# A feed-forward that begins with its narrow column group instead of a wide one

## The chip, the cores and the metric

One NeuronCore of one Trainium2 chip runs the whole program. The metric is device time in microseconds (us) of one execution, lower is better. The engines are named as in the profile: PE is TensorE (matmuls; its weight loads are PEld), DVE is VectorE, ACT is ScalarE, POOL is GpSimd, SP is SyncE, which issues most of the DMAs.

## What is computed

Two decoder layers over 256 tokens of width 1024, in float32. The change touches the feed-forward alone, with `D_FF` = 2816 columns:

```python
def swiglu(h, w_gate_up, w_down):
    gu = h @ w_gate_up
    gate, up = jnp.split(gu, [D_FF], axis=-1)
    return (jax.nn.silu(gate) * up) @ w_down

...
        h = h + hybrid_mixer(rmsnorm(h, norm_mix_w[l]), w_in[l], ret_out[l], conv_w[l], conv_b[l],
                             dt_bias[l], a_log[l], d_skip[l], ssd_norm_w[l], ssd_out[l], w_o[l])
        h = h + swiglu(rmsnorm(h, norm_ffn_w[l]), w_gate_up[l], w_down[l])
```

The mixer ends with the product `merged @ w_o`, so the feed-forward's input is `h` plus that product, normalised.

## The kernel before

Every float32 product is made of three matmuls of a rounded type: each operand is split into a high part (`wh`, `xh`), which ScalarE rounds, and a low part (`wl`, `xl`), which VectorE gets by subtraction. `mm3` (lines 542 to 545) issues high by high, high by low, low by high. All weights go through this: a piece of 128 x 1024 elements is loaded by SP, rounded by ScalarE (line 506) and subtracted by VectorE (line 527). There are seven buffers for split pieces (`HB` = 7).

The 256 tokens are two tiles of 128, t0 and t1. The normalised input stands transposed in `xT`, in two halves of 512 features, each with its high and low part.

The 2816 columns of the feed-forward are groups `c` = 0 to 4 of 512 and group 5 (`NPAIR`) of 256, each for the gate and for the up product. There are three ways to compute a group:

- tokens stationary (`tm_jobs`, `tm_pair`, lines 824 and 859): the stationary operand is a block of `xT`, the weights stream past, the result has tokens as rows. A step `(m, t, k)` is one `mm3` for member `m` (0 gate, 1 up), token tile `t` and row block `k` of 8. The result has to be transposed on TensorE (`transposed`, line 631) for the product that follows.
- weights stationary (`fm_job`, line 970, lines 988 to 991): a block of weights is stationary and the high and low parts of all tokens stream past, 512 columns, then 256 columns against the low weights. The result is already transposed; its two halves are added by ScalarE and VectorE (`gathered`).
- "seven" (`wino_job`): a Strassen-like product with seven instead of eight blocks, tokens stationary, whose weight sums are made on VectorE and by DMAs. It needs sums of `xT`, which `seven_sums` makes on VectorE in the first part of the feed-forward (tiles `plain` and `D`).

The table `FFN` sets the order of the groups: tokens stationary for 0, then 1 (weights stationary), 2 (seven), 3 (weights stationary), 4 (seven), 5 (weights stationary), then the down projection `out_wino`. The first entry is not done by the general job but by `tm_pair`, whose order of steps is

```python
(m, t, k) for t in range(NT) for m, n in ((0, 8), (1, 4)) for k in range(n)
```

and after that the last four `k` of up for both tiles. So it begins with t0 alone: 8 steps of gate and 4 of up.

Ahead of it stands the output projection (`out_job` with `head=8 - TAIL`), which finishes one accumulator after another, that of t1's second half last. After each, `add_to(norm)` adds it to `h`; `Norm.half` makes the sum of squares (`square`: ScalarE, line 776), the reciprocal root (`power`: GpSimd, line 655), the normalised rows `xn` in a `sil` tile (VectorE, line 744, in the trace L233), their transposes (TensorE, line 640) and the split into `xT` (ScalarE, then VectorE). t1's part of this runs while the feed-forward's first matmuls of t0 do.

The order of instructions on each engine is fixed when the program is built: `Flow` is a small event model in the kernel that takes, on each engine, the ready operation with the lowest priority number, by costs and latencies written in it. The hardware then runs each engine's list in that order.

`gate_post` applies the silu to the gate (ScalarE), `up_post` multiplies by up (VectorE), transposes and splits into `gu`, the operand of the down projection, which asks for its groups in the order 0, 3, 4, 5, with the two groups 1 and 2 as a seven in between.

Of the kernel before, what the change touches and what calls it, by code (L numbers as in the profile page):

```python
# [11 lines left out]
AF = mybir.ActivationFunctionType  # L12
ALU = mybir.AluOpType
# [3 lines left out]
P = 128  # L17
D = 1024
SEQ = 256
NT = 2  # L20
# [7 lines left out]
NPAIR = FF // 512  # L28
C_Q, C_K, C_V, C_G, C_Z, C_X, C_DT, C_GR, C_GS = 0, 1024, 2048, 4096, 6144, 8192, 11264, 11296, 12320
NB = 24  # L30

GF = (1, 3, NPAIR)


DW = 1
# [157 lines left out]
def trunk_kernel(  # L193
# [8 lines left out]
    SLOW, MT_SLACK = 1500.0, 800.0  # L202
# [17 lines left out]
    def act(n, pr, out, in_, func, psum=False, **kw):  # L220
        ptr = sum(hasattr(kw.get(a), "shape") for a in ("scale", "bias"))
        cost = 0.833 * n + (50 if psum else 92) + 93 * ptr + (95 if "accum_out" in kw else 0)
        return Op("act", cost, lambda: nc.scalar.activation(out=out, in_=in_, func=func, **kw),  # L223
                  pr, TABLES.get(func))
# [4 lines left out]
    def tt(n, pr, out, in0, in1, op):  # L229
        return dve(n, pr, lambda: nc.vector.tensor_tensor(out=out, in0=in0, in1=in1, op=op))  # L230
# [593 lines left out]
    def tm_jobs(xT, members, order):  # L824

        first, pe_pr = take(len(members))
        acc, left = {}, {}
        for m, t, k in order:
            post, n, kper = members[m]
            j = first + m  # L830
            if k == 0:
                yield accS
            yield xT.when(k, t)
            wh, wl = yield jobs[j][k // kper]

            def emit():
                if not started[0]:
                    started[0] = True

                    idle[0].pr, idle[0].cost, idle[0].fn = -10, 0.0, lambda: None  # L840
                if k == 0:
                    acc[m, t] = new_acc()
                xh, xl, _ = xT.at(k // 4)
                tsl = slice(t * P, (t + 1) * P)
                mm3(acc[m, t][:, :n], xh[:, k % 4, tsl], xl[:, k % 4, tsl], wh[:, k % kper, :], wl[:, k % kper, :], k == 0, k == 7)

            yield pe(3 * mm_cost(n), pe_pr + 0.5, emit)
            left[m, k // kper] = left.get((m, k // kper), NT * kper) - 1
            if not left[m, k // kper]:
                fl.release(hlS)  # L850
            if k == 7:
                fl.spawn(post(t, acc[m, t], j, accS))
# [3 lines left out]
        return tm_jobs(xT, [(post, n, kper)], [(0, t, k) for t in range(NT) for k in range(lead)]  # L856
                       + [(0, t, k) for k in range(lead, 8) for t in range(NT)])

    def tm_pair(xT, *members):

        return tm_jobs(xT, members, [(m, t, k) for t in range(NT) for m, n in ((0, 8), (1, 4)) for k in range(n)]
                       + [(1, t, k) for k in range(4, 8) for t in range(NT)])

    GOT = ("a", "b", "c1", "c2", "u1", "u2", "u3")

# [191 lines left out]
    def out_wino(op, nk, at, tag, order, post, add, ops):  # L1057
# [74 lines left out]
        for t in range(NT):  # L1132
# [6 lines left out]

    FFN = [[("plain", 0)],
           [("fm", 1)],
           [("seven", (2,), ("t3", "t4"))],
           [("fm", 3)],
           [("seven", (4,), ("t3", "t4"))],
           [("fm", NPAIR)]]
    DIRECT = ()
    DOWN_APART = ()

# [14 lines left out]
    def add_layer_jobs(l):  # L1165
        def srcs_of(kind, *at):
            if kind == "gr":
                return tm_srcs(w_gr[l, at[0]])
            if kind in FM:
                return fm_srcs(w_fm[l, FM[kind] + at[0] + (at[0] + at[1] if len(at) > 1 else 0)])  # L1170
            if kind in ("ret", "ssd", "wo"):
                return out_srcs({"ret": ret_out, "ssd": ssd_out, "wo": w_o}[kind][l])
            return tm_srcs(w_tm[l, TM[kind] + at[0]], kper=1 if l == 0 and (kind, *at) == ("v", 0) else 2)

        def adds_of(kind, *at, order=MIXED):
            if kind == "seven":
                c = TM[at[0]] + at[1]
                return [sevens(w_tm[l, c], w_tm[l, c + 1], added=at[2], order=order, slots=None)]
            return [plain((srcs_of(kind, *at), APARTS.get((kind, *at), ())))]

        for m in MIXERS[l]:
            if m == ("ret",):
                group(sevens(w_rw[l, 0], w_rw[l, 1], added=("t3", "t4"), order=RMID, first=RET_FIRST),
                      plain((out_srcs(ret_out[l])[8:], RET_APART)))
            elif m == ("ssd",):
                group(sevens(w_sw[l, 0], w_sw[l, 1], added=("t3", "t4"), order=SMID, slots=(ccS, new_cc)),
                      plain((out_srcs(ssd_out[l])[8:], ())))
            elif isinstance(m, tuple):
                for add in adds_of(*m, order=ALONE):
                    group(add)  # L1190
            else:
                group(*(chain(*(a for j in stream for a in adds_of(*j))) for stream in m))
        for members in FFN:
            adds = []
            for kind, *at in members:
                if kind == "seven":
                    adds.append(chain(*(sevens(w_gate_up[l, 0, c], w_gate_up[l, 1, c], added=at[1], order=ALONE if len(members) == 1 else ASIDE,
                                               slots=(ccS, new_cc)) for c in at[0])))
                elif kind == "fm":
                    adds.append(plain(*((srcs, APART) for c in at for srcs in gf_srcs(l, c))))  # L1200
                else:
                    adds.append(plain(*((srcs, APART) for c in at for srcs in gate_up_srcs(l, c))))
            group(*adds)
        lone = [s for k, s in enumerate(out_srcs(w_down[l])) if k // 4 not in (DW, DW + 1)]
        group(sevens(w_dw[l, 0], w_dw[l, 1], added=("t3", "t4"), order=AMID, slots=(ccS, new_cc)),
              plain((lone, DOWN_APART)))
# [24 lines left out]
    def layer(l, mix, nxt, opening=None):  # L1231
# [696 lines left out]

        gu = Operand(NPAIR + 1, ["A", "C", "Y", "A", "C", "Y"])

        def gate_post(sg_ev):
            def post(t, ps, j, sem):
                yield silS
                s = new_sil()
                yield act(512, j, s, ps, AF.Silu, psum=sem is accS)
                fl.release(sem)
                fl.set(sg_ev[t], s)
            return post

        def up_post(sg_ev, c):  # L1940
            def post(t, ps, j, sem):
                s = yield sg_ev[t]
                yield tt(512, j, s, ps, s, ALU.mult)
                fl.release(sem)
                yield from transposed(s, 4, gu, c, t, j, slack=SLOW)
                fl.release(silS)
            return post

# [48 lines left out]
                makers += [((lambda p=p, job=job: job(ffn.xT, p)), 1) for p in (gate, up)]  # L1997
            return makers

        def pair(c):  # L2000
            sg_ev = [Event() for _ in range(NT)]
            return gate_post(sg_ev), up_post(sg_ev, c)

        def ffn_jobs(kind, *at):
            if kind == "seven":
# [5 lines left out]
        last = max(i for i, g in enumerate(FFN) for kind, *_ in g if kind == "seven")  # L2011
        for i, members in enumerate(FFN):
            if i == 0:
                yield from tm_pair(ffn.xT, *((m, 512, 2) for m in pair(members[0][1])))
            else:
                yield from together(*[ffn_jobs(*m) for m in members])
            if i == last:
                ffn.drop_sums()
# [202 lines left out]
```

## Time and profile before

| | before |
|---|---|
| time, median of 3 runs | 1253.2 us (1253.19 to 1253.69) |
| the profiled execution | 1253.21 us, span 1251.4 us |
| mean granted TensorE clock | 0.999 |
| PE busy | 1241.9 us, 99% |
| DVE busy | 1108.2 us, 89% |
| ACT busy | 882.7 us, 71% |
| DMA | 266.27 MB, mean 213 GB/s |

The span runs from the first to the last instruction; 1.8 us of the time lie outside it. A matmul's shown duration covers its way through the array and overlaps the next one, so the pace of matmuls is read from start to start. "Idle before, releaser" behind a row says how long the engine stood and which instruction ended that.

### The profile page before, as it was taken

Reading aid. Unit: us, or ns where it says so; the run is one execution under the profiler, and the core shown is the slowest. Engines: PE = TensorE matmul, PEld = TensorE weight load, DVE = VectorE, ACT = ScalarE, POOL = GpSimd, SP = SyncE. Lnnn points to the kernel's source line nnn. Section 1 sums busy time; section 2 is a strip of 40 time slices with the busy share of each in tenths; the row PEclk is TensorE's granted clock in tenths of the full one; section 3 lists DMA queues with packets and bytes.
Section 4 is the critical chain, followed back from the end, with each engine's and each line's share of the span. In section 5 each row is a group of like instructions: output and inputs, shape, how many; then the busy total and the mean of one; then the engine's idle time right before and its main releaser. Section 6 shows DMA issues by size and latency. Waiting matters only on the chain.

```text
span 1251.4 us, 17609 instructions
## 1 busy us (share of the span) xinstructions
PE 1241.9 (99%) x6286; PEld 1052.4 (84%) x6286; DVE 1108.2 (89%) x1516; ACT 882.7 (71%) x1305; POOL 71.1 (6%) x92
## 2 busy tenths in 40 slices
PE   9999999999999999999999999999999999999997
PEld 8889888888888888888888898888888888888886
DVE  6998989789999979999788888888899998899995
ACT  6866876977776666776586676878877674776753
POOL 0000000001012001001000000000010110010000
PEclk9999999999999999999999999999999999999999
DMA  8758555456768658877776475555577786688872
GB/s 293 248 146 284 184 180 174 153 194 192 253 238 226 229 178 231 297 212 219 249 257 227 124 256 167 188 172 163 208 186 234 243 234 213 225 209 249 289 204 86
DMA packets 76343, 266.27 MB, mean 213 GB/s; under 512 B 8768, under 2 KB 9024, under 8 KB 76256
## 3 DMA queue, kind: packets, MB, share of 16 engines
q1 hardware_dynamic: 68416, 237.25, 55.7%
q0 software_dynamic: 7552, 27.38, 11.8%
q8 instruction: 49, 0.80, 0.2%
q10 hardware_dynamic: 288, 0.52, 0.1%
q14 instruction: 38, 0.31, 0.1%
HBM read 262.96 MB, written 2.16 MB: 212 GB/s over the span
## 4 chain that ended last, share of the span: by engine, by line
PE 92%; ACT 3%; issue 2%; DMA 1%; DVE 0%; POOL 0%; SPq 0%; POOLq 0%; ACTq 0%
PE acc L543 19%; PE acc L544 19%; PE acc L545 19%; PE acc L988 15%; PE acc L989 9%; PE tr L640 2%; PE yps L1700 2%; PE acc L991 2%; ACT wh L506 1%; ACT seg L1668 1%; PE acc L1422 1%; PE tr L1593 1%; PE ips L1687 1%; DMA raw<-in_w_tm_dram 1%; DMA raw<-in_w_gr_dram 0%
## 5 line engine op out<-in xcount | busy, mean ns | idle before, releaser
L506 ACT ACTIVATE wh<-raw 128x1024 fp32r<-128x1024 f32 (+2 forms) x388 | 397.0, 1035 | 150.6 <-PE acc L545 36.3
L527 DVE TENSOR_TENSOR wl<-raw,wh 128x1024 fp32r<-128x1024 f32 (+2 forms) x388 | 458.9, 1196 | 48.5 <-ACT wh L506 46.6
L988 PE MATMUL acc<-xT,wh 128*128 128x512 f32 x840 | 304.2, 400 | 0.0
L989 PE MATMUL acc<-xT,wl 128*128 128x256 f32 x960 | 251.6, 281 | 0.0
L543 PE MATMUL acc<-wh,xT 128*128 128x512 f32 (+1 forms) x568 | 220.6, 388 | 0.0
L545 PE MATMUL acc<-wh,xT 128*128 128x512 f32 (+1 forms) x568 | 216.1, 380 | 0.0
L544 PE MATMUL acc<-wl,xT 128*128 128x512 f32 (+1 forms) x568 | 216.1, 380 | 0.0
L989 PEld LDWEIGHTS acc<-xT,wl 128*128 128x128 f32 x960 | 181.2, 189 | 10.1
L988 PEld LDWEIGHTS acc<-xT,wh 128*128 128x128 f32 x840 | 158.0, 188 | 32.2
L544 PEld LDWEIGHTS acc<-wl,xT 128*128 128x128 f32 x568 | 106.7, 188 | 20.4 <-issue 1.2
L543 PEld LDWEIGHTS acc<-wh,xT 128*128 128x128 f32 x568 | 106.7, 188 | 19.8 <-issue 1.6
L545 PEld LDWEIGHTS acc<-wh,xT 128*128 128x128 f32 x568 | 106.6, 188 | 19.5
L506 ACT ACTIVATE wh<-raws 128x1024 fp32r<-128x1024 f32 x80 | 83.5, 1056 | 31.7 <-DVE raws L230 12.5
L527 DVE TENSOR_TENSOR wl<-raws,wh 128x1024 fp32r<-128x1024 f32 x80 | 96.4, 1222 | 8.9 <-ACT wh L506 8.7
L543 PE MATMUL acc<-wh,A 128*128 128x512 f32 x224 | 89.8, 401 | 0.2
L545 PE MATMUL acc<-wh,A 128*128 128x512 f32 x224 | 87.4, 390 | 0.0
L544 PE MATMUL acc<-wl,A 128*128 128x512 f32 x224 | 87.3, 390 | 0.0
L233 DVE SCALAR_TENSOR_TENSOR cc<-cc,cv 128x255 f32<-128x255 f32 (+1 forms) x144 | 67.3, 479 | 3.0 <-ACT cc L223 2.1
L543 PE MATMUL acc<-wh,C 128*128 128x512 f32 (+1 forms) x152 | 59.2, 389 | 0.0
L544 PE MATMUL acc<-wl,C 128*128 128x512 f32 (+1 forms) x152 | 58.3, 384 | 0.2 <-DVE wl L527 0.2
L545 PE MATMUL acc<-wh,C 128*128 128x512 f32 (+1 forms) x152 | 58.2, 383 | 0.0
L223 ACT ACT_TABLE_LOAD x41 | 52.6, 1283 | 6.1 <-DVE cc L233 5.4
(197 smaller groups left out, 2006.8 us busy)
## 6 DMA issues: line engine op xcount, KB each, us to landing
raw<-in_w_tm_dram SPq DMA_DIRECT2D x104, 512.0 KB, 4.2
raw<-in_w_fm_dram SPq DMA_DIRECT2D x80, 512.0 KB, 4.3
raw<-in_w_gf_dram SPq DMA_DIRECT2D x40, 512.0 KB, 4.5
raw<-in_w_gate_up_dram SPq DMA_DIRECT2D x32, 512.0 KB, 5.8
raw<-in_w_down_dram SPq DMA_DIRECT2D x28, 512.0 KB, 4.5
raw<-in_w_gr_dram SPq DMA_DIRECT2D x24, 352.0 KB, 3.7
seg<-acs SPq DMA_DIRECT2D x16, 512.0 KB, 4.9
raw<-in_ret_out_dram SPq DMA_DIRECT2D x16, 512.0 KB, 4.3
```

The lines of the kernel that those rows point to most:

```text
L223: return Op("act", cost, lambda: nc.scalar.activation(out=out, in_=in_, func=func, **kw), pr, TABLES.get(func))
L233: return Op("dve", 1.04 * n + 130, lambda: nc.vector.scalar_tensor_tensor(out=out, in0=in0, scalar=scalar, in1=in1, op0=op0, op1=op1), pr)
L506: nc.scalar.activation(out=wh[:, :m], in_=raw[:, :m], func=AF.Copy)
L527: nc.vector.tensor_tensor(out=wl[:, :m], in0=raw[:, :m], in1=wh[:, :m].bitcast(F32), op=ALU.subtract)
L543: nc.tensor.matmul(ps, lhsT=lh, rhs=rh, start=first, stop=False, **kw)
L544: nc.tensor.matmul(ps, lhsT=lh, rhs=rl, start=False, stop=False, **kw)
L545: nc.tensor.matmul(ps, lhsT=ll, rhs=rh, start=False, stop=last, **kw)
L640: nc.tensor.transpose(out=ps[:, j * P : (j + 1) * P], in_=src[:, j * P : (j + 1) * P], identity=ident)
L988: nc.tensor.matmul(a, lhsT=wh[:, k % 4, fsl], rhs=x[:, k % 4, :, :], start=k == 0, stop=False)
L989: nc.tensor.matmul(a[:, :SEQ], lhsT=wl[:, k % 4, fsl], rhs=xh[:, k % 4, :], start=False, stop=False)
L991: nc.tensor.matmul(a, lhsT=wh[:, k % 4, fsl], rhs=x[:, k % 4, :, :], start=False, stop=True)
L1700: nc.tensor.matmul(ps[:, i * HD : (i + 1) * HD], lhsT=sg[:, i, :], rhs=xdt[:, i * HD : (i + 1) * HD], start=True, stop=True)
```

## The change

The feed-forward's first entry becomes group 5 (256 columns), tokens stationary, all 8 `k` of gate and of up for t0 and then for t1 (`lead=8`). Its weights come in pieces of four `k` by 256 columns (`kper` 4), two for gate and two for up. Group 0 becomes a weights-stationary group of 512 columns in second place, and groups 1 and 3 move back by one place of their kind. The weights of group 0 are laid out for that on the host (`GF`). `gate_post` and `up_post` take the width.

```diff
-GF = (1, 3, NPAIR)
+GF = (0, 1, 3, NPAIR)
...
-    def tm_pair(xT, *members):
-
-        return tm_jobs(xT, members, [(m, t, k) for t in range(NT) for m, n in ((0, 8), (1, 4)) for k in range(n)]
-                       + [(1, t, k) for k in range(4, 8) for t in range(NT)])
+    def tm_pair(xT, *members, lead=4):
+
+        return tm_jobs(xT, members, [(m, t, k) for t in range(NT) for m, n in ((0, 8), (1, lead)) for k in range(n)]
+                       + [(1, t, k) for k in range(lead, 8) for t in range(NT)])
...
-    FFN = [[("plain", 0)],
+    FFN = [[("rows", NPAIR)],
+           [("fm", 0)],
+           [("seven", (2,), ("t3", "t4"))],
            [("fm", 1)],
-           [("seven", (2,), ("t3", "t4"))],
-           [("fm", 3)],
            [("seven", (4,), ("t3", "t4"))],
-           [("fm", NPAIR)]]
+           [("fm", 3)]]
...
-                elif kind == "fm":
+                elif kind in ("fm", "rows"):
                     adds.append(plain(*((srcs, APART) for c in at for srcs in gf_srcs(l, c))))
...
-        def gate_post(sg_ev):
+        def gate_post(sg_ev, n=512):
             def post(t, ps, j, sem):
                 yield silS
-                s = new_sil()
-                yield act(512, j, s, ps, AF.Silu, psum=sem is accS)
+                s = new_sil()[:, :n]
+                yield act(n, j, s, ps[:, :n], AF.Silu, psum=sem is accS)
...
-        def up_post(sg_ev, c):
+        def up_post(sg_ev, c, n=512):
             def post(t, ps, j, sem):
                 s = yield sg_ev[t]
-                yield tt(512, j, s, ps, s, ALU.mult)
+                yield tt(n, j, s, ps[:, :n], s, ALU.mult)
                 fl.release(sem)
-                yield from transposed(s, 4, gu, c, t, j, slack=SLOW)
+                yield from transposed(s, n // P, gu, c, t, j, slack=SLOW)
...
-                yield from tm_pair(ffn.xT, *((m, 512, 2) for m in pair(members[0][1])))
+                yield from tm_pair(ffn.xT, *((m, 256, 4) for m in pair(members[0][1], 256)), lead=8)
```

TensorE's list in layer 0, where the feed-forward passes from t0 to t1. `sil_4500` and `sil_4501` (in the new program `sil_4524` and `sil_4525`) are the two halves of `xn` of t1. Before:

```order
L545 MATMUL acc_4503<-wh_4456,xT_4397 128x512
L640 MATMUL tr_4515<-cst_78,sil_4500 128x128 x4
L543 MATMUL acc_4503<-wh_4467,xT_4397 128x512
L544 MATMUL acc_4503<-wl_4478,xT_4397 128x512
L545 MATMUL acc_4503<-wh_4467,xT_4397 128x512
L640 MATMUL tr_4524<-cst_78,sil_4501 128x128 x4
L543 MATMUL acc_4503<-wh_4467,xT_4397 128x512
L544 MATMUL acc_4503<-wl_4478,xT_4397 128x512
L545 MATMUL acc_4503<-wh_4467,xT_4397 128x512
L543 MATMUL acc_4536<-wh_4329,xT_4397 128x512
```

And in the changed program:

```order
L544 MATMUL acc_4487<-wl_4450,xT_4402 128x256
L545 MATMUL acc_4487<-wh_4436,xT_4402 128x256
L640 MATMUL tr_4533<-cst_78,sil_4524 128x128 x4
L640 MATMUL tr_4542<-cst_78,sil_4525 128x128 x4
L543 MATMUL acc_4552<-wh_4329,xT_4397 128x256
L544 MATMUL acc_4552<-wl_4337,xT_4397 128x256
L545 MATMUL acc_4552<-wh_4329,xT_4397 128x256
```

`acc_4503` was the up product of t0 and `acc_4536` the gate of t1; now they are `acc_4487` and `acc_4552`. The transposes stood after ten of t0's twelve steps, with the two last steps behind them; now both blocks stand behind all sixteen steps of t0 and directly ahead of t1.

VectorE's list in the same place. L527 are weight splits, L238 the statistics of the norm, L233 `xn`. Before:

```order
L230 TENSOR_TENSOR O_3866<-O_3866,acc_4293 128x512
L527 TENSOR_TENSOR wl_4472<-raw_4344,wh_4456 128x1024
L527 TENSOR_TENSOR wl_4478<-raw_4355,wh_4467 128x1024
L238 TENSOR_SCALAR ms_4466<-ss_4465,ms_4413 128x1
L527 TENSOR_TENSOR wl_4495<-raw_4434,wh_4485 128x1024
L233 SCALAR_TENSOR_TENSOR sil_4500<-O_3866,rstd_4491,wb_3938 128x512
L233 SCALAR_TENSOR_TENSOR sil_4501<-O_3866,rstd_4491,wb_3938 128x512
L230 TENSOR_TENSOR xT_4397<-tr_4515,xT_4397 128x4x128
```

And in the changed program:

```order
L230 TENSOR_TENSOR O_3866<-O_3866,acc_4293 128x512
L527 TENSOR_TENSOR wl_4478<-raw_4344,wh_4459 128x1024
L527 TENSOR_TENSOR wl_4492<-raw_4355,wh_4476 128x1024
L238 TENSOR_SCALAR ms_4475<-ss_4474,ms_4413 128x1
L527 TENSOR_TENSOR wl_4519<-raw_4434,wh_4503 128x1024
L233 SCALAR_TENSOR_TENSOR sil_4524<-O_3866,rstd_4512,wb_3938 128x512
L233 SCALAR_TENSOR_TENSOR sil_4525<-O_3866,rstd_4512,wb_3938 128x512
L230 TENSOR_TENSOR sil_4486<-acc_4487,sil_4486 128x256
L230 TENSOR_TENSOR xT_4397<-tr_4533,xT_4397 128x4x128
```

The chain of t1 and the three splits between its parts stand as before; the product of gate and up of t0 (`sil_4486`) is new between `xn` and the split of the transposes.

ScalarE's list there, the square of the norm, the split of the seventh piece and the silu of t0's gate. Before:

```order
L223 ACTIVATE sil_4464,ss_4465<-O_3866 128x512
L506 ACTIVATE wh_4485<-raw_4434 128x1024
L223 ACTIVATE sil_4502<-acc_4443 128x512
L223 ACTIVATE xT_4397<-tr_4515 128x4x128
L223 ACTIVATE xT_4402<-tr_4524 128x4x128
```

And in the changed program:

```order
L223 ACTIVATE sil_4473,ss_4474<-O_3866 128x512
L223 ACTIVATE sil_4486<-acc_4443 128x256
L506 ACTIVATE wh_4503<-raw_4434 128x1024
L223 ACTIVATE xT_4397<-tr_4533 128x4x128
L223 ACTIVATE xT_4402<-tr_4542 128x4x128
```

The silu moved ahead of the split. Behind the feed-forward's opening, TensorE has 64 matmuls of the weights-stationary kind more in each layer and four transposes less; the down projection and the next layer stand as before.

## Rows read from the trace of the kernel before

**Rows 1.** The page, part 1: busy us (share of the span) and instructions.

```profile
PE 1241.9 (99%) x6286; PEld 1052.4 (84%) x6286; DVE 1108.2 (89%) x1516; ACT 882.7 (71%) x1305; POOL 71.1 (6%) x92
```

**Rows 2.** Waits of PE, 449.5 to 640 us: total us, times, longest.

```profile
PE tr L640 <- DVE sil L233: 0.3, 1, 0.3
```

**Rows 3.** Stretches: length, then busy of PE, PEld, DVE, ACT, POOL; clock, DMA.

```profile
449.16:458.71 9.55, 9.26 (x46) 7.46 (x44) 7.86 (x11) 6.36 (x12) 1.57 (x1) 1.00 0.78 263
458.71:472.33 13.62, 13.62 (x61) 11.26 (x60) 12.33 (x15) 10.83 (x15) 0.00 (x0) 1.00 0.60 189
...
495.75:514.80 19.05, 19.05 (x86) 15.77 (x84) 19.04 (x21) 15.73 (x19) 0.88 (x1) 1.00 0.79 220
514.80:538.20 23.40, 23.40 (x138) 20.48 (x136) 21.17 (x26) 15.32 (x23) 2.60 (x3) 1.00 0.88 271
...
557.24:569.36 12.12, 12.12 (x73) 10.68 (x72) 9.91 (x12) 8.68 (x13) 0.00 (x0) 1.00 0.98 373
```

**Rows 4.** Timeline of PE in the opening, layer 0: start, duration, instruction.

```profile
449.16 0.39 PE L543 MATMUL acc<-wh,xT 128*128 128x512 f32 x1
449.39 0.39 PE L544 MATMUL acc<-wl,xT 128*128 128x512 f32 x1
...
456.42 0.63 PE L640 MATMUL tr<-cst,sil 128*128 128x128 f32 x4 [0.29 <-DVE sil L233]
...
458.71 0.40 PE L543 MATMUL acc<-wh,xT 128*128 128x512 f32 x1
```

**Rows 5.** Timeline of PE in the opening of layer 1.

```profile
1074.18 0.63 PE L640 MATMUL tr<-cst,sil 128*128 128x128 f32 x4 [0.29 <-DVE sil L233]
```

**Rows 6.** The chain of work that ended last, 453 to 459 us.

```profile
455.52 0.76 DVE sil L233
456.28 0.14 issue
...
457.74 0.44 PE tr L640 x4
```

**Rows 7.** Timeline of POOL: the power of t0 and of t1.

```profile
443.45 0.56 POOL L243 TENSOR_TENSOR rstd<-ms,mhalf 128x1 f32<-128x1 f32 x1 [44.28 <-DVE ms L238]
453.91 1.57 POOL L243 TENSOR_TENSOR rstd<-ms,mhalf 128x1 f32<-128x1 f32 x1 [9.90 <-DVE ms L238]
```

**Rows 8.** Timeline of DVE, from the opening on.

```profile
449.42 1.23 DVE L527 TENSOR_TENSOR wl<-raw,wh 128x1024 fp32r<-128x1024 f32 x1
...
451.35 2.36 DVE L527 TENSOR_TENSOR wl<-raw,wh 128x1024 fp32r<-128x1024 f32 x2
...
453.85 1.22 DVE L527 TENSOR_TENSOR wl<-raw,wh 128x1024 fp32r<-128x1024 f32 x1
...
457.72 0.69 DVE L230 TENSOR_TENSOR xT<-tr,xT 128x512 fp32r<-128x512 f32 x1 [0.78 <-ACT xT L223]
...
476.52 0.42 DVE L230 TENSOR_TENSOR sil<-acc,sil 128x256 f32<-128x256 f32 x1
```

**Rows 9.** Timeline of ACT, from the opening on.

```profile
452.13 0.64 ACT L223 ACTIVATE sil<-O 128x512 f32<-128x512 f32 x1
...
452.75 1.07 ACT L506 ACTIVATE wh<-raw 128x1024 fp32r<-128x1024 f32 x1
...
475.77 0.39 ACT L223 ACTIVATE sil<-acc 128x256 f32<-128x256 f32 x1 [0.45 <-PE acc L991]
```

**Rows 10.** Timeline of PE: 256 columns with weights stationary, 352 with tokens stationary.

```profile
475.11 0.40 PE L989 MATMUL acc<-xT,wl 128*128 128x256 f32 x2
475.34 0.40 PE L991 MATMUL acc<-xT,wh 128*128 128x512 f32 x1
...
634.55 0.32 PE L545 MATMUL acc<-wh,xT 128*128 128x352 f32 x1
634.71 0.32 PE L543 MATMUL acc<-wh,xT 128*128 128x352 f32 x1
```

**Rows 11.** Timeline of DVE: the first split for the first seven, layer 0.

```profile
480.40 1.23 DVE L527 TENSOR_TENSOR wl<-raws,wh 128x1024 fp32r<-128x1024 f32 x1
```

More of the change, by code (lines that the diff above doesn't have):

```diff
@@ L1998, in fm_pair, with pair @@
             return makers
-        def pair(c):
+        def pair(c, n=512):
             sg_ev = [Event() for _ in range(NT)]
-            return gate_post(sg_ev), up_post(sg_ev, c)
+            return gate_post(sg_ev, n), up_post(sg_ev, c, n)
         def ffn_jobs(kind, *at):
```

## The prediction

> **What bounds the kernel now.** I read the page's first part: TensorE is busy 99% of the span and VectorE 89% [rows 1]. "Busy" says little where the ends of matmuls are modelled, so I next asked which waits TensorE has in the feed-forward of layer 0, from its second matmul at 449.5 us into the next layer: one, the transposes of `xn` waiting for VectorE, 0.3 us [rows 2]. Then the times stage by stage [rows 3]: the opening pair (columns 0 to 511, tokens stationary) runs from 449.16 to 472.33, 23.17 us; a feature-major pair of 512 columns takes 23.40; a Strassen-like "seven" takes 19.05 for 84 matmuls, 226.8 ns each; the last pair of 256 columns takes 12.12. A matmul of 512 columns in an unhindered stream starts 0.23 us after the one before [rows 4], so the sevens hold no wait either. The reader should take from this: a matmul more or a wait more is added to the end time, and outside the opening there is no TensorE wait that could pay it back.
>
> The opening is the one place where TensorE meets a latency. The output projection `w_o` ends at 449.16; only then can the second token tile (t1) be added to `h`, squared, normalised, transposed and split. Until then TensorE has only matmuls of the first token tile (t0). Before: 12 steps of three 512-column matmuls. They last until shortly before 456.42, where the transposes of t1 wait [rows 4]. The matmuls of t1 begin at 458.71. Layer 1 has the same wait of 0.29 us [rows 5]. So that cover fits the latency almost exactly, and the question is what the change does to either.
>
> **The latency.** Followed backwards: the transposes at 456.42 [rows 4], `xn` on VectorE at 455.52 [rows 6], the power on GpSimd at 453.91 [rows 7], the statistics on VectorE just ahead of it, behind two weight splits from 451.35 [rows 8], the square on ScalarE at 452.13 [rows 9]. The new order of VectorE has the same rows up to `xn`, with the same three splits among them (the weights differ, not their size), so this end stays. Two things are put in. On ScalarE the silu of t0's gate (256 columns, 0.39 [rows 9]) now stands ahead of the third split, which ran at 452.75; the split would start about 453.2 and end about 454.3, and VectorE's half of it runs from about 454.35 instead of 453.85, 1.22 long, until about 455.55. `xn` stands behind it, so it starts at about 455.6 instead of 455.52. On VectorE a product of 256 columns (0.42 [rows 8]) stands between `xn` and the split of the transposes; that split starts at 457.72, over 0.7 after `xn` is through, so the product fits in between.
>
> The power took 1.57 us here, in a time when VectorE was splitting, and 0.56 at 443.45 when VectorE was idle [rows 7]. It now starts with VectorE idle for some 0.4 us. I take 0.1 us for what may come of it; if it is stretched over the later split it costs 0.4 more, and if it is short nothing is won, since the split stands ahead of `xn` anyway. (The Trainium skill, SBUF — State Buffer, section "SBUF: two separate sides", says that GpSimd and a VectorE operation with two inputs in SBUF share a port pair under an exclusive lock, and that whichever starts first blocks the other. The 1.57 beside the 0.56 agrees; by that rule the power would go first now and the split would lose about 0.1 us, which is the value taken.)
>
> So the transposes come at about 456.5. From their start in the trace to the split of their result at 457.72, 0.69 long, and the third matmul of a step, the first to read the low part, it is 458.41 plus the 0.14 that [rows 6] show between VectorE and TensorE: 458.55. The first two matmuls of the step fit ahead of it. t1 effectively starts at 458.55 − 0.23 + 0.1, about 458.45; I use 458.5. Before, it was 458.71, set by TensorE itself.
>
> **The cover.** After the change t0 has 16 steps of three matmuls of 256 columns. The trace has no such stream with tokens stationary. The nearest rows: two 256-column matmuls in a row with weights stationary, 0.23 for two, 0.115 each; and 352 columns with tokens stationary, 0.16 each, less 96 columns at 2.4 GHz (0.04), 0.12 each [rows 10]. I take 0.116: 48 matmuls are 5.6 us (5.5 to 5.8). The cover ends at about 454.75, where it lasted almost to 456.4 before with 8.2 us of matmuls (36 × 0.227). The weights for it are split early enough: its fourth and last piece is the one that VectorE splits at 449.42 [rows 8], through at 450.65 and needed at about 453.3. TensorE then stands about 1.8 us before the transposes and about 1 us between them and t1, in sum 458.5 − 449.16 − 5.6 − 0.9 (two blocks of four transposes, 0.44 each [rows 6]) = 2.85 us, where it stood about 0.45.
>
> **The sum, for one layer.** Opening: 9.34 to t1, then 48 matmuls of t1, 5.6: 14.95 instead of 23.17, so −8.2. Against that the feature-major pair of 256 columns becomes one of 512: 23.40 − 12.12 = +11.3 [rows 3]. The transposes behind the opening are two blocks of two instead of two of four: −4 × 0.11 = −0.45 [rows 6]. Together +2.6 us. In words: 2.4 us of new standing time at the opening (2.85 − 0.45), −0.45 of transposes, and the rest, about 0.6, for the same columns in more and shorter matmuls. Two layers: +5.2.
>
> **What is hidden.** The weights are as many bytes and as many splits as before. VectorE does one half pair more in the feature-major form and half the posts in the other: 16 short operations instead of 10, about 1.5 us per layer, and as much on ScalarE; both lie under TensorE unless the cushion goes (second rival). The first split of the first seven is done at 481.6 [rows 11] for a matmul at 495.75 [rows 3], a cushion of 14 us. The last feature-major pair is now `gu[3]`; the down projection asks for it only after its first four k steps and the first seven product, 60 matmuls or 13.6 us later, against a handful of short operations (0.42 and 0.69 each [rows 8]) in its last posts.
>
> The profiled run took 1253.21 us, the median of the runs 1253.2, so one can stand for the other; +5.2 gives 1258.4.
>
> **Rivals.** *The clock falls in the new wait (0.08).* The granted clock reads 1.00 in every stretch [rows 3], and the longest idle of TensorE in the feed-forwards is 0.29 us [rows 4, 5], so the trace doesn't show what 2.85 us in pieces do. If TensorE went to 1.2 GHz for the 48 matmuls of t1, each would need 256/1.2 = 213 ns, an estimate, +0.097 each, +4.7 per layer: about 1267.8. It speaks against it that the standing time is broken by transposes. The Trainium skill (TensorE: Matmul & The Clock Gate, section "What's actually happening") makes the low level the default that activity lifts; no run here yet shows it returning.
>
> *VectorE falls behind (0.06).* Its work in the opening shrinks by four splits of 1.22 and by 1.1 of posts, 6.0 us, TensorE's time by 8.2; so it enters the rest 2.2 us later relative to TensorE, and in the sevens it is busy 19.04 of 19.05 [rows 3]. If there were no cushion that would cost 2.2 per layer: 1262.8. It needs the cushion of 14 us to be gone first.
>
> *The latency itself shortens (0.04).* If the power took 0.56 and `xn` followed it without the split, t1 would come 1.0 us earlier per layer: 1256.4. The order of VectorE speaks against it.
>
> *Not slower: the sevens give it back (0.06).* VectorE has no idle time there. If it paces them, a TensorE that arrives 2.6 us late finds more weights ready, runs them closer, and the end stays at about 1253.3. This decides if TensorE's starts in the two sevens of a layer hold at least 2.6 us of hidden waits. They hold none that I find: 226.8 ns a matmul against 0.227 in the opening.
>
> **How the numbers follow.** The forecast gets 0.76. Its own bounds per layer: t1 at 458.3 with 0.115 a matmul gives +2.3, t1 at 458.9 (the stretched power) with 0.12 gives +3.2; so 1257.9 to 1259.6. With the shorter latency below, and part of the second rival above, 1256.4 to 1261.5 leaves out under 2 in 10. A change of this kernel can be told from none at about 0.2%, 2.5 us. Slower by more than that: the forecast and the first three rivals, 0.93. Within it 0.05, faster 0.02, both from the last.
>
> **What would show it.** Right: in both layers the transposes of t1 wait for `xn` about 1.5 to 2 us and t1's first step about 1 us more for VectorE or ScalarE; the opening's matmuls end some 15 us after its start; the sevens still take 19.05, the down projection starts about 2.6 us later; 120 matmuls more. Wrong: 256-column matmuls spaced well above 0.12; `xn` in another place than about 455.6; a clock below 1.00 behind the wait; weights waited for in the first feature-major pair or in the sevens.

## The result, and the profile after

Over five runs each, the changed kernel takes 1258.7 us (1257.7 to 1258.9), the kernel before 1253.7 (1253.2 to 1254.0). The ratio is 1.0037, with an interval of 1.0026 to 1.0049: slower, by 5.0 us. The forecast was 1258.4, counted from 1253.2 for the kernel before. The profiled execution took 1258.68 us, its span 1256.9, at a mean granted clock of 0.999.

The page's first part shows 120 matmuls more, as the forms demand, and 2.7 us more of busy TensorE, against a span that is 5.5 us longer [rows 1]:

```profile
PE 1244.6 (99%) x6406; PEld 1058.1 (84%) x6406; DVE 1110.9 (88%) x1528; ACT 885.8 (70%) x1317; POOL 69.0 (5%) x92
```

TensorE's waits in the feed-forward of layer 0. The transposes' wait has grown from 0.3 to 1.1 us, and one has come behind it [rows 2]:

```profile
PE tr L640 <- DVE sil L233: 1.1, 1, 1.1
PE acc L545 <- DVE xT L230: 0.2, 1, 0.2
```

The windows by stage (the stretch and its length; then busy time and count of PE, PEld, DVE, ACT and POOL; the granted clock, the DMA share, GB/s), to be held against [rows 3]. The first two are the opening with its two token tiles, then come the first weights-stationary group, a seven, a weights-stationary group, a seven, a weights-stationary group:

```profile
449.96:458.75 8.79, 7.66 (x59) 6.84 (x57) 7.92 (x12) 5.99 (x11) 0.55 (x1) 1.00 0.83 276
458.75:464.61 5.86, 5.63 (x48) 5.62 (x47) 4.58 (x7) 5.19 (x8) 0.00 (x0) 1.00 0.21 60
464.61:487.61 23.00, 23.00 (x135) 20.06 (x133) 21.88 (x31) 14.75 (x23) 2.60 (x3) 1.00 0.82 248
487.61:506.67 19.06, 19.06 (x86) 15.77 (x84) 19.04 (x21) 15.73 (x19) 0.88 (x1) 1.00 0.78 217
506.67:530.10 23.43, 23.43 (x138) 20.50 (x137) 21.20 (x26) 15.36 (x23) 2.60 (x3) 1.00 0.86 272
530.10:549.14 19.04, 19.04 (x85) 15.77 (x84) 19.03 (x21) 15.72 (x19) 0.86 (x1) 1.00 0.77 213
549.14:572.54 23.40, 23.40 (x137) 20.48 (x136) 18.29 (x24) 15.48 (x23) 0.86 (x2) 1.00 0.89 318
```

From the opening to the down projection it is 572.54 − 449.96 = 122.58 us, where it was 569.36 − 449.16 = 120.20 [rows 3]: +2.38. The opening takes 14.65 for 23.17, 8.5 less, and the rest takes 10.9 more. From the transposes of t1 in layer 0 to those in layer 1 (the rows of 456.95 and 1077.08 in the next fence) it is 1077.08 − 456.95 = 620.13, before 617.76 [rows 4, 5]: +2.37 again. Two layers make 4.7 of the 5.5 by which the profiled span is longer; the rest is already there when the first feed-forward starts (449.96 for 449.16), in a part of the program that the change leaves alone.

TensorE's timeline at the opening (start, duration, instruction; in brackets the idle time before it and what ended that):

```profile
449.96 0.28 PE L543 MATMUL acc<-wh,xT 128*128 128x256 f32 x1
...
455.60 0.28 PE L545 MATMUL acc<-wh,xT 128*128 128x256 f32 x1
456.95 1.29 PE L640 MATMUL tr<-cst,sil 128*128 128x128 f32 x8 [1.08 <-DVE sil L233]
458.27 0.38 PE L543 MATMUL acc<-wh,xT 128*128 128x256 f32 x1
458.49 0.28 PE L544 MATMUL acc<-wl,xT 128*128 128x256 f32 x1
458.99 0.38 PE L545 MATMUL acc<-wh,xT 128*128 128x256 f32 x1 [0.23 <-DVE xT L230]
...
464.61 0.38 PE L640 MATMUL tr<-cst,sil 128*128 128x128 f32 x2
...
1077.08 1.29 PE L640 MATMUL tr<-cst,sil 128*128 128x128 f32 x8 [1.07 <-DVE sil L233]
```

The rows show t0's 48 matmuls in a closed row, 47 intervals in 5.64 us, 0.12 each; then nothing for TensorE to do; then both blocks of transposes; then t1's first step with gaps in it. The brackets name only the idle time between modelled ends. What the opening loses is found from starts: 14.65 − 96 × 0.12 − 8 × 0.11 = 2.25 us, of which the brackets show 1.31. Some 1.2 of it lie ahead of the transposes (456.95 less the end of t0's stream, 449.96 + 48 × 0.12 = 455.72), 1.0 between them and t1's steady row.

The chain that sets the transposes, from the timeline of ScalarE, of VectorE and of GpSimd; VectorE's last row is the first split of the first seven:

```profile
453.54 0.40 ACT L223 ACTIVATE sil<-acc 128x256 f32<-128x256 f32 x1
453.81 1.08 ACT L506 ACTIVATE wh<-raw 128x1024 fp32r<-128x1024 f32 x1
...
452.14 2.36 DVE L527 TENSOR_TENSOR wl<-raw,wh 128x1024 fp32r<-128x1024 f32 x2
454.42 0.21 DVE L238 TENSOR_SCALAR ms<-ss,ms 128x1 f32<-128x1 f32 x1
454.92 1.23 DVE L527 TENSOR_TENSOR wl<-raw,wh 128x1024 fp32r<-128x1024 f32 x1 [0.29 <-ACT wh L506]
456.06 1.41 DVE L233 SCALAR_TENSOR_TENSOR sil<-O,rstd,wb 128x512 f32<-128x512 f32 x2
...
458.25 1.36 DVE L230 TENSOR_TENSOR xT<-tr,xT 128x512 fp32r<-128x512 f32 x2 [0.44 <-ACT xT L223]
...
472.53 1.22 DVE L527 TENSOR_TENSOR wl<-raws,wh 128x1024 fp32r<-128x1024 f32 x1
...
454.70 0.55 POOL L243 TENSOR_TENSOR rstd<-ms,mhalf 128x1 f32<-128x1 f32 x1 [9.89 <-DVE ms L238]
```

The power on GpSimd is through at 455.25. `xn` starts at 456.06 without a wait, at the end of the third weight split: VectorE's order now sets it, by 0.8 us, and no longer GpSimd.

### The profile page after: what moved, and what is told of

It is laid out like the page before. It is cut to its first block, busy times and chain, and to the rows that moved or that the text cites. A ratio compares the mean times of both kernels' runs of the same rounds, so it can differ in the third digit from the quotient of the medians.

```text
span 1256.9 us, 17871 instructions
## 1 busy us (share of the span) xinstructions
PE 1244.6 (99%) x6406; PEld 1058.1 (84%) x6406; DVE 1110.9 (88%) x1528; ACT 885.8 (70%) x1317; POOL 69.0 (5%) x92
## 4 chain that ended last, share of the span: by engine, by line
PE 90%; ACT 5%; DVE 2%; issue 2%; DMA 1%; SPq 0%; POOLq 0%; POOL 0%; ACTq 0%
PE acc L543 19%; PE acc L545 19%; PE acc L544 18%; PE acc L988 15%; PE acc L989 9%; PE yps L1700 2%; PE acc L991 2%; PE tr L640 2%; ACT wh L506 2%; ACT seg L1668 1%; DVE wl L527 1%; PE acc L1422 1%; PE tr L1593 1%; DMA raw<-in_w_gr_dram 1%; PE ips L1687 1%
## 5 line engine op out<-in xcount | busy, mean ns | idle before, releaser
L527 DVE TENSOR_TENSOR wl<-raw,wh 128x1024 fp32r<-128x1024 f32 (+2 forms) x388 | 459.1, 1196 | 53.5 <-ACT wh L506 51.6
L988 PE MATMUL acc<-xT,wh 128*128 128x512 f32 x896 | 324.2, 399 | 0.1
L989 PE MATMUL acc<-xT,wl 128*128 128x256 f32 x1024 | 268.3, 281 | 0.0
L543 PE MATMUL acc<-wh,xT 128*128 128x512 f32 (+2 forms) x568 | 213.6, 376 | 0.0
L545 PE MATMUL acc<-wh,xT 128*128 128x512 f32 (+2 forms) x568 | 209.5, 369 | 0.5 <-DVE xT L230 0.5
L544 PE MATMUL acc<-wl,xT 128*128 128x512 f32 (+2 forms) x568 | 209.3, 368 | 0.0
L989 PEld LDWEIGHTS acc<-xT,wl 128*128 128x128 f32 x1024 | 193.3, 189 | 10.8
L988 PEld LDWEIGHTS acc<-xT,wh 128*128 128x128 f32 x896 | 168.5, 188 | 34.7 <-PE acc L991 0.4
L527 DVE TENSOR_TENSOR wl<-raws,wh 128x1024 fp32r<-128x1024 f32 x80 | 96.4, 1222 | 10.0 <-ACT wh L506 9.6
L233 DVE SCALAR_TENSOR_TENSOR cc<-cc,cv 128x255 f32<-128x255 f32 (+1 forms) x144 | 67.3, 479 | 3.0 <-ACT cc L223 2.1
```

The source lines that it names most:

```text
L233: return Op("dve", 1.04 * n + 130, lambda: nc.vector.scalar_tensor_tensor(out=out, in0=in0, scalar=scalar, in1=in1, op0=op0, op1=op1), pr)
L527: nc.vector.tensor_tensor(out=wl[:, :m], in0=raw[:, :m], in1=wh[:, :m].bitcast(F32), op=ALU.subtract)
L543: nc.tensor.matmul(ps, lhsT=lh, rhs=rh, start=first, stop=False, **kw)
L544: nc.tensor.matmul(ps, lhsT=lh, rhs=rl, start=False, stop=False, **kw)
L545: nc.tensor.matmul(ps, lhsT=ll, rhs=rh, start=False, stop=last, **kw)
L988: nc.tensor.matmul(a, lhsT=wh[:, k % 4, fsl], rhs=x[:, k % 4, :, :], start=k == 0, stop=False)
```

## The experiments

The theory: t0's matmuls of 256 columns end before t1's normalisation is through, and what TensorE stands there is most of the loss. Against it stand three others: that the new order of groups costs something (the narrow group second, three wide ones), that the form does (256 columns with tokens stationary, 120 matmuls more), and that the clock does. The runs of the kernel before beside the first four have a median of 1253.9, beside the last three 1253.8.

**The order alone.** The kernel before, with its wide opening, and the narrow group weights stationary as before but in second place:

```diff
     FFN = [[("plain", 0)],
+           [("fm", NPAIR)],
+           [("seven", (2,), ("t3", "t4"))],
            [("fm", 1)],
-           [("seven", (2,), ("t3", "t4"))],
-           [("fm", 3)],
            [("seven", (4,), ("t3", "t4"))],
-           [("fm", NPAIR)]]
+           [("fm", 3)]]
```

> The kernel before with its opening untouched (columns 0 to 511, tokens stationary) and only the weights-stationary groups moved: the narrow group second, groups 1 and 3 after it, the wide one last, as in the changed kernel. Theory of the standing time (the change costs 2.4 us per layer because t0's shorter matmuls no longer cover the norm of t1): no change, 1253.7 within 0.7. Rival of the placing (VectorE enters the sevens with a smaller cushion, or the wide group ahead of the down projection costs): 2 us per layer or more, 1257 to 1259.

Measured: 1253.6 (1252.8 to 1254.6), ratio 0.9999 (0.9990 to 1.0008). TensorE's only wait in the feed-forward is the old one, 0.3 us. The order of the groups costs nothing.

**A shorter cover.** The changed kernel with `lead=4`: t0 has 12 steps instead of 16 ahead of the transposes, and the four others come at the end. The same matmuls, 12 of them moved behind the wait.

```diff
-... pair(members[0][1], 256)), lead=8)
+... pair(members[0][1], 256)), lead=4)
```

> The changed kernel with four steps of up for t0 ahead of t1 instead of eight; the matmuls are the same in number and shape. Theory of the standing time: t0's cover shrinks from 48 to 36 matmuls of 0.12 us, t1 starts when it did, so 1.44 us more per layer, 1258.7 + 2.9 = 1261.6. Rival of the form (the extra time is the price of more and shorter matmuls, wherever they stand): unchanged, 1258.7 within 0.7.

Measured: 1263.9 (1263.2 to 1264.3), ratio 1.0080 (1.0067 to 1.0092). It is 10.0 above the kernel before, 2.2 more than expected. TensorE's timeline:

```profile
453.79 0.28 PE L545 MATMUL acc<-wh,xT 128*128 128x256 f32 x1
456.59 1.56 PE L640 MATMUL tr<-cst,sil 128*128 128x128 f32 x8 [2.52 <-DVE sil L233]
...
459.01 0.41 PE L543 MATMUL acc<-wh,xT 128*128 128x256 f32 x1
459.22 0.41 PE L544 MATMUL acc<-wl,xT 128*128 128x256 f32 x1
...
460.92 0.28 PE L543 MATMUL acc<-wh,xT 128*128 128x256 f32 x1
461.03 0.28 PE L544 MATMUL acc<-wl,xT 128*128 128x256 f32 x1
```

The wait grows from 1.08 to 2.52, by 1.44, which is twelve matmuls of 0.12: the latency stays where it was, the cover is shorter by just what was moved. That part is as the theory has it, 2.9 us in two layers. The surplus is the clock. The wait of layer 1, and the windows at the end of the wait and behind it in each layer (columns as above):

```profile
1079.05 1.94 PE L640 MATMUL tr<-cst,sil 128*128 128x128 f32 x8 [2.52 <-DVE sil L233]
...
457.48:460.90 3.42, 3.42 (x16) 3.04 (x15) 2.08 (x3) 2.05 (x4) 0.00 (x0) 0.50 0.52 199
460.90:466.67 5.77, 5.77 (x50) 5.77 (x49) 4.46 (x5) 4.50 (x6) 0.00 (x0) 1.00 0.40 136
1078.70:1085.50 6.80, 6.45 (x28) 6.03 (x29) 3.26 (x6) 3.71 (x6) 0.00 (x0) 0.50 0.38 140
1085.50:1090.34 4.84, 4.84 (x42) 4.84 (x41) 4.26 (x5) 3.19 (x5) 0.00 (x0) 1.00 0.58 209
```

The granted clock is at 0.50, the level of 1.2 GHz, for 3.42 and 6.80 us, and matmuls start 0.21 us apart instead of 0.12. In layer 0 it falls 0.9 us after the transposes have started, in layer 1 still in the wait, 0.35 us ahead of them.

**The shorter cover, filled.** The same kernel with 20 matmuls of 256 columns, whose result nothing reads, in the place of the wait:

```diff
     def tm_jobs(...):
+            if fill and (m, t, k) == fill:
+                yield accS
+                def idle_mm():
+                    a = new_acc("idle")
+                    xh = xT.at(0)[0]
+                    for i in range(20):
+                        nc.tensor.matmul(a[:, :256], lhsT=xh[:, i % 4, :P], rhs=wh[:, i % kper, :], ...)
+                yield pe(20 * mm_cost(256), pe_pr + 0.5, idle_mm)
+                fl.release(accS)
...
-... lead=4)
+... lead=4, fill=(1, 0, 3))
```

> The changed kernel with four steps of up for t0 ahead of t1, as in e2_lead4, and 20 matmuls of 256 columns more into a spare accumulator that nothing reads, in the time in which TensorE stood ahead of the transposes of t1 (20 x 0.12 = 2.4 of about 2.7 us). They add work and no result. Theory that the granted clock fell in e2_lead4 because TensorE stood so long: the clock stays at 1.00 and the time falls to 1261.6, what the shorter cover alone costs. Rival that the 2.2 us above 1261.6 have another cause: no faster than 1263.8, or slower by the added work.

Measured: 1261.4 (1260.6 to 1263.1), ratio 1.0059 (1.0046 to 1.0073), as expected. TensorE's timeline shows the fill and, directly behind it, the transposes; the two windows run from the transposes to the first matmul of group 0, in layer 0 and in layer 1:

```profile
454.55 2.56 PE L860 MATMUL idle<-wh,xT 128*128 128x256 f32 x20
457.23 1.29 PE L640 MATMUL tr<-cst,sil 128*128 128x128 f32 x8
...
459.28 0.38 PE L545 MATMUL acc<-wh,xT 128*128 128x256 f32 x1 [0.23 <-DVE xT L230]
...
457.23:466.33 9.10, 8.81 (x68) 8.17 (x69) 7.04 (x9) 6.89 (x10) 0.00 (x0) 1.00 0.48 166
1080.00:1089.10 9.10, 8.82 (x69) 8.17 (x69) 7.02 (x9) 6.89 (x10) 0.00 (x0) 1.00 0.53 180
```

Work that gives nothing takes 2.5 us off, 1263.9 − 1261.4, because the clock now stays at 1.00 behind it. The profiles place the gain in the two openings: from the first matmul of t0 to the first of group 0 they take 16.09 and 15.89 us here, 17.07 and 18.28 without the fill, 3.4 less in sum. This profile is of the slowest of the five executions, which loses 1.5 us elsewhere, between the two openings. So a fall of the clock is a real price of such a wait, but not one that the changed kernel pays: its clock is 1.00 in each stretch of the opening, and from 1070.10 to 1085.00 in layer 1.

**The latency taken out from under the splits.** In the changed kernel, three weight splits of group 0 stand on VectorE between the residual addition for t1 and `xn`. Here all splits of group 0 wait until the first half of t1 is in `xT`. Nothing else is edited, but `Flow` then places t1's transposes earlier in TensorE's list, after 13 and 14 of t0's 16 steps.

```diff
-    def splitter(turn, k, n, ev, job, src, sem):
+    def splitter(turn, k, n, ev, job, src, sem, hold=None):
         def land(raw, landed):
             yield landed
+            if hold:
+                yield hold
             wh, wl = yield from split_piece(raw, k * n, turn, job - 0.7, src)
...
-                    adds.append(plain(...))
+                    adds.append(plain(..., hold=holds[l] if (kind, *at) == ("fm", 0) else None))
...
+        def held():
+            yield ffn.xT.ready[0][1]
+            fl.set(holds[l])
+        fl.spawn(held())
```

> The changed kernel with one thing added: the weight splits of the second group wait until the first half of t1's transposed input is split, so that three splits leave ScalarE and VectorE free for the norm of t1. Theory of the standing time: the norm's chain loses the two splits ahead of its statistics and the one ahead of xn, the third matmul of t1's first step comes about 2.1 us earlier (6.9 us after the opening's start instead of 9.0), TensorE hardly stands, 2.1 per layer come back: 1258.7 - 4.2 = 1254.5. Rival of the form: unchanged, 1258.7. If the held splits come too late for the second group instead, TensorE waits at its start and the time stays at 1256 or more.

Measured: 1253.6 (1252.3 to 1255.3), ratio 0.9996 (0.9987 to 1.0005): all of the 5 us is back, where 4.2 were expected. TensorE has no wait in the feed-forward of layer 0. The windows of its opening and of the first weights-stationary group:

```profile
448.65:461.02 12.37, 12.37 (x105) 12.37 (x104) 9.51 (x15) 9.14 (x16) 0.55 (x1) 1.00 0.38 129
461.02:483.99 22.97, 22.97 (x134) 20.06 (x133) 22.97 (x32) 15.28 (x24) 1.74 (x2) 1.00 0.90 295
```

The opening takes 12.37 instead of 14.65, and that is all its matmuls: 96 × 0.12 + 8 × 0.11 = 12.4. The next group has the held splits beside it, VectorE full, and is no longer for that. VectorE's timeline shows the chain without splits in it:

```profile
450.05 0.68 DVE L230 TENSOR_TENSOR O<-O,acc 128x512 f32<-128x512 f32 x1
451.53 0.21 DVE L238 TENSOR_SCALAR ms<-ss,ms 128x1 f32<-128x1 f32 x1 [0.79 <-ACT sil L223]
452.40 1.41 DVE L233 SCALAR_TENSOR_TENSOR sil<-O,rstd,wb 128x512 f32<-128x512 f32 x2 [0.66 <-POOL rstd L243]
```

`xn` starts 3.75 us after the opening, 6.10 in the changed kernel.

**The first two splits left.** The same with the first two splits of group 0 left where they were (`past=2`: the hold applies to the pieces past the second). Of the three in t1's chain only the third is held.

> The changed kernel with only the third of the three splits held until the first half of t1's transposed input is split; the two ahead of the statistics stay. Theory: xn, which started at the end of that split (456.06), follows the power (454.70 + 0.55) instead and starts at about 455.3; t1 comes 0.75 us earlier per layer: 1258.7 - 1.5 = 1257.2. Rival that the split costs xn nothing: unchanged, 1258.7.

Measured: 1257.1 (1256.3 to 1257.5), ratio 1.0026 (1.0017 to 1.0036), as expected. In VectorE's timeline `xn` waits for GpSimd again:

```profile
455.31 1.42 DVE L233 SCALAR_TENSOR_TENSOR sil<-O,rstd,wb 128x512 f32<-128x512 f32 x2 [0.66 <-POOL rstd L243]
```

The opening began at 449.98, so `xn` comes after 5.33 us, 0.77 sooner than in the changed kernel; two layers make 1.5, and the time falls by 1.6.

**The form in the old place.** The kernel before with its last group of 256 columns computed as the change does it, tokens stationary, but left at the end:

```diff
-           [("fm", NPAIR)]]
+           [("rows", NPAIR)]]
...
+            if kind == "rows":
+                return [((lambda m=m: tm_job(ffn.xT, m, 256, 4)), 1) for c in at for m in pair(c, 256)]
```

> The kernel before with its opening untouched and the narrow group still last, but computed with tokens stationary, so that the form of the changed kernel's opening stands where nothing has to be covered. Theory of the standing time: 96 matmuls of 0.12 us and four transposes of 0.11, 11.96 us, against 11.28 for the weights-stationary form, 0.7 per layer: 1253.7 + 1.4 = 1255.1. Rival of the form: the whole 2.5 per layer, 1258.7.

Measured: 1256.8 (1255.0 to 1258.1), ratio 1.0022 (1.0012 to 1.0033), 1.7 more than expected. The windows of this group and of the down projection:

```profile
557.42:569.79 12.37, 12.37 (x105) 12.36 (x104) 9.44 (x11) 7.87 (x11) 0.00 (x0) 1.00 0.98 366
569.79:629.26 59.47, 59.09 (x267) 48.25 (x265) 51.31 (x61) 34.60 (x43) 4.59 (x6) 1.00 0.72 208
```

The group takes 12.37 for 12.12 [rows 3]. The down projection behind it takes 59.47, where the same window of the kernel before has 58.08 (569.36 to 627.44): most of the layer's 1.64 us arise there. TensorE's timeline shows two places in it where TensorE is late, by about 0.3 and 0.4 us:

```profile
573.52 0.44 PE L640 MATMUL tr<-cst,sil 128*128 128x128 f32 x2
...
592.85 0.50 PE L543 MATMUL acc<-wh,D 128*128 128x512 f32 x1 [0.24 <-ACT sx L223]
```

Four transposes more are another 0.44; they come with the form wherever it stands. The first place is the transposes of the form's own result, and layer 1 shows what they wait for (VectorE's rows, then TensorE's):

```profile
1189.50 1.23 DVE L230 TENSOR_TENSOR raws<-raws,cc 128x1024 f32<-128x1024 f32 x1 [2.85 <-DMA cc<-in_w_dw_dram]
...
1193.64 0.42 DVE L230 TENSOR_TENSOR sil<-acc,sil 128x256 f32<-128x256 f32 x1
...
1194.11 0.44 PE L640 MATMUL tr<-cst,sil 128*128 128x128 f32 x2 [1.31 <-DVE sil L230]
```

The product of gate and up stands on VectorE behind a sum of weights that waits for its DMA, 2.85 us here and 0.51 in layer 0, and TensorE, already in the down projection, waits for the product. That is the order of the rows; no run took it away. The second place, behind an operation on ScalarE, was not followed up. So this run doesn't price the form alone. The run with all splits held does it better: there the form stands in the opening with no wait left, and costs nothing that the times can tell.

**The hold in the kernel before.** The theory says that the old wait of 0.29 us per layer has the same cause. The seventh and eighth piece of the opening, which t0 doesn't need, are held in the kernel before (`past=6`); the split of the seventh is the one that stands between t1's statistics and `xn` [rows 8].

> The kernel before with one thing added: the seventh and eighth weight pieces of its opening, which t0 doesn't need, are split only after the first half of t1's transposed input. Theory that t1's norm is delayed by the splits beside it: without the third split the power takes 0.56 us instead of 1.57, xn starts about 1.0 earlier, and the 0.45 us that TensorE stands ahead of the transposes goes, in each layer: 1253.7 - 0.9 = 1252.8. Rival that xn's place is set by something else: unchanged, 1253.7.

Measured: 1252.8 (1251.9 to 1255.1), ratio 0.9995 (0.9986 to 1.0004), 1.0 us below the kernel before and not to be told from it by the times. The trace tells more: there is no wait of TensorE in the feed-forward, and the opening of layer 1 follows that of layer 0 after 617.21 us (450.62 to 1067.83) instead of 617.77 (449.16 to 1066.93). From GpSimd's, VectorE's and TensorE's timeline:

```profile
455.37 0.55 POOL L243 TENSOR_TENSOR rstd<-ms,mhalf 128x1 f32<-128x1 f32 x1 [9.90 <-DVE ms L238]
...
455.95 1.41 DVE L233 SCALAR_TENSOR_TENSOR sil<-O,rstd,wb 128x512 f32<-128x512 f32 x2 [0.67 <-POOL rstd L243]
...
457.19 0.39 PE L548 MATMUL acc<-wh,xT 128*128 128x512 f32 x1
457.43 1.03 PE L643 MATMUL tr<-cst,sil 128*128 128x128 f32 x8
```

The power takes 0.55 instead of 1.57 us, and `xn` starts 5.33 us after the opening instead of 6.36. The transposes follow the matmul ahead of them 0.24 us after its start, without a gap. Of all the kernels here this has the lowest time, but none is shown to be faster than the kernel before.

## Why the prediction was right, point by point

**The mechanism is shown.** Most of the loss, 1.8 of 2.4 us per layer, is t1's latency, for which the matmuls of t0 no longer suffice. Moving twelve matmuls from the cover to behind the wait lengthened the wait by twelve matmuls; taking work out of the latency gave the time back, in part for one split and in full for three. The order of the groups, the first rival theory, costs nothing that the times can tell. That the sum came so near is in part luck: its two main terms were off by 0.6 and 0.4 us per layer, one too large and one too small, and the kernel before measured 0.5 us more than the 1253.2 that the forecast started from.

**The latency** was taken too long. The prediction put `xn` 6.44 us after the opening's start (455.6 against 449.16); it came after 6.10, and before it had come after 6.36. First, the silu of t0's gate was to delay VectorE's half of the third split by 0.5 us. It delayed it by 0.27: that half began 4.96 us after the opening's start, before 4.69 [rows 8]; ScalarE's rows show its half of the split beginning ahead of the end shown for the silu. Second, the split was counted with its whole shown length, and `xn` a little behind it, 1.25 us from start to start. It was 1.14, as between the two splits of the 2.36 us row in [rows 8]. Then the 0.14 us between VectorE and t1's third matmul was 0.05 (458.25 + 0.69 = 458.94, to 458.99), and 458.45 was rounded up to 458.5. That `xn` would wait for the split and not for a short power was right. The power took 0.55 instead of 1.57 [rows 7]. Before, `xn` had waited for the long power; now it follows the split, 0.26 sooner than before. t1's matmuls end as if their stream had begun at 8.9 (464.61 less 48 × 0.12, less 449.96), where the prediction had 9.34. The standing time was foretold as 1.5 to 2 us ahead of the transposes and about 1 behind them; it is 1.2 and 1.0. Of the kernel before the prediction says that 36 matmuls, 8.2 us, lasted almost to the transposes; 30 did, until 455.97 (449.16 + 30 × 0.227), and six stood between and behind the two blocks. Its sum goes by the opening's start and t1's, so nothing in it hangs on that.

The Trainium skill (SBUF — State Buffer, section "SBUF: two separate sides") gave the right sign for the power: where GpSimd starts first it isn't held up, and 0.55 agrees. That the split then loses something doesn't show: it began at 454.92, 0.22 us behind the power and 0.33 ahead of its end, and took 1.23, as at other places. There the trace differs from the page, and the measurement decides.

**The pace** was at its upper bound, 0.12 instead of 0.116: 0.2 us more for t1's 48 matmuls. It offsets over a third of the error in the latency, so that the opening came out at 14.65 for 14.95.

**The sum for one layer**, term by term: new standing time 2.25 − 0.45 = 1.8, predicted 2.4; transposes −0.45, as predicted; more and shorter matmuls +1.0 by difference (2.38 − 1.8 + 0.45), predicted 0.6. Rows bear the 1.0 out: the wide group takes 23.40 weights stationary, 23.17 less the 0.45 of waits in the old opening, so +0.7; the narrow one takes 12.37 for 12.12 in the run with the form in the old place, so +0.25. The 0.4 that the prediction lacked is its pace, 96 × 0.004. Together 2.4 for 2.6, and 4.7 in the trace for 5.2. The runs' medians are 5.0 apart. The kernel with held splits checks the two last terms: without any standing time it should be above the kernel before by 1.0 − 0.45 less the 0.45 that stood before, 0.1 per layer; it was level within its interval.

**What was hidden stayed hidden.** The first seven's first split is done at 473.75 (VectorE's row at 472.53, 1.22 long) for a matmul at 487.61, a cushion of 13.9 us: VectorE doesn't fall behind. The sevens take 19.06 and 19.04 for 19.05: they give nothing back. The stretch from the down projection's first matmul to the next layer's first takes 58.06 (572.54 to 630.60) where it took 58.08, so the wide group at the end doesn't hold it up.

**The clock** as a rival was near. In the changed kernel it stays, behind 1.08 and 0.23 us of shown idle time; with 2.52 us in one piece it falls, and falling costs the 2.5 us that the filled run brings back in both layers together. The prediction's price for it, 4.7 us per layer, took the low level for the whole of t1; it lasted 3.4 and 6.8 us.

## What to carry to other kernels

Where a stream of matmuls is there to cover a latency, count both in microseconds before making the stream narrower: a matmul of half the columns covers about half the time, 0.12 us for 0.227 here. When the cover no longer suffices, look first at what stands in the latency's way on the other engines: work that is not due yet (here weight splits for the next group) can be held behind the chain, which gave all of the 5 us back. And an operation that is released by the later of two chains gains when that one is shortened, up to the other: the power became 1.0 us shorter and `xn` came 0.26 sooner. Ask for both ends before writing down what is won.

## What was not expected of the hardware

An idle time of TensorE of 2.52 us came with 3.42 us at the level of 1.2 GHz in one layer, from 0.9 us behind its end, and with 6.80 us in the other, from 0.35 us ahead of its end, for the same list of instructions; one of 1.08 us came with none. Twenty matmuls of no use in its place kept the clock at 1.00. The Trainium skill (TensorE: Matmul & The Clock Gate, section "What's actually happening") has the low level as the default that activity lifts, which agrees with the return of the clock in both layers.

The power of one column on GpSimd took 1.57 us where a split on VectorE had started just ahead of it [rows 7, 8], and 0.55 in the changed kernel and in those with the splits held, where none had.

In nine profiles the first feed-forward began between 448.65 and 450.62 us, behind a part of the program that is the same in all. A single profile of this kernel is therefore uncertain by about 1 us before the change is reached, and differences of one layer were read from marks inside it.
